# Masked softmax on one core: an empty first turn around the work of VectorE and ScalarE

## The chip, the core and the metric

The kernel runs on one core of a Trainium2 chip. The core has five engines with an instruction stream each: TensorE (PE), VectorE (DVE), ScalarE (ACT), GpSimd (POOL) and SyncE (SP), and 16 DMA engines that move data between the chip's memory (HBM) and the core's own. The engines run on their own and wait for each other on semaphores. The metric is the time of one execution on the device in microseconds; the median of several runs is compared.

## The reference

The input x has 16 batches of 8 heads x 256 x 256 numbers in float32, and each batch has a length between 128 and 255. The softmax goes along the last axis over the first `length` columns; the other columns of the result are zero.

```python
result = np.zeros_like(x)
for b in range(batch):
    length = lengths[b]
    masked = x[b, :, :, :length].copy()
    masked = masked - np.max(masked, axis=-1, keepdims=True)
    exp_masked = np.exp(masked)
    result[b, :, :, :length] = exp_masked / np.sum(exp_masked, axis=-1, keepdims=True)
```

## The kernel before

A batch is 2048 rows of 256 columns, held as 128 partitions x 16 rows x 256 (2 MB). Eight such slots stand in `xt`, and batch number b (in the kernel's own order) uses slot b modulo 8. Each slot is worked on in place: it is loaded, masked, exponentiated, divided and stored.

**The start.** ACT's queue loads the 16 lengths (L139), SP's queue the first batch in two halves (L142). POOL makes a row of column numbers, `iota_i` (L177), two vectors of ones and two zeros. DVE turns the column numbers into `down` (L225), casts the lengths (L230), PE spreads them over the partitions with a small matmul (L210), and DVE scales them into `len_s` (L233). POOL waits for both of DVE's steps, clears the right part of one slot (L187), then issues the loads of the next three batches (L192) and clears three slots more.

**Loads.** From batch 4 on, a loop on POOL (L197 to L205) reads a batch's length and picks, over nested branches, a load as wide as the length needs (L164); it waits for the load before last, and for the store that frees the slot.

**DVE.** Its stream is written out: `begin`-like steps L223 to L237, then the masks of batch 0 (`mask`, L242), then for each batch `divide` of the first half, the mask of the next batch, `divide` of the second half. `mask` waits for the load and takes the minimum of x and a ramp that is huge and negative behind the length (a `scalar_tensor_tensor` of 128 x 2048); `divide` waits for a half batch of exponentials, takes the reciprocal of the row sums (L263) and multiplies (L266). Masks count on the semaphore `s_min`, half batches of exponentials on `s_exp`, divided halves on `s_out`.

**ACT.** After one exponential on a zero, which brings its table in (`warm`, L342), a loop of two turns (L345) has the work of eight batches written out in its body: for each batch 16 exponentials of 128 x 256, each with its row sum (L354), 128 in a turn. The exponentials wait for `s_min` at a value computed from the turn (L349, L351).

**Stores.** SP waits for `s_out` and stores a batch in one to four parts (L145 to L153). Before the second store it waits for the third mask (L148).

**The end.** DVE checks all row sums for values out of range (L298 to L309); a slower path stands behind a branch (L314 on DVE, L361 on ACT) and isn't taken here. SP waits for the last store.

The lines that the change touches are SP's wait L148, the start of DVE's stream (L223 to L237), its main loop (L273 to L285), and ACT's warm-up and loop (L342 to L357).

Of the kernel before, what the change touches and what calls it, by code (L numbers as in the profile page):

```python
# [9 lines left out]
F32 = mybir.dt.float32  # L10
BF16 = mybir.dt.bfloat16
I32 = mybir.dt.int32
ALU = mybir.AluOpType
AX = mybir.AxisListType.X
EXP = mybir.ActivationFunctionType.Exp
DVE = mybir.EngineType.DVE
ACT = mybir.EngineType.Activation
# [4 lines left out]
def kernel(  # L22
# [6 lines left out]
    nc = tc.nc  # L29
    P = nc.NUM_PARTITIONS  # L30

    batch, heads, seq_q, seq_k = x.shape
    rows = heads * seq_q
    assert rows % P == 0
    nt = rows // P
    half = nt // 2
# [8 lines left out]
    slots = 8  # L45
# [3 lines left out]
    def batch_of(pos):  # L49
        return pos + 1 if pos < ahead - 1 else {ahead - 1: 15, 15: 0}.get(pos, pos)  # L50
# [5 lines left out]
    big = 1.0e30  # L56

    def parts(b):


        if b == 0:
            cuts = [0, 2, quarter, half, nt]
        elif b < 8:
            cuts = [0, half, half + quarter, nt]
        elif b < 13 or b == batch - 1:
            cuts = [0, half, nt]
        else:
            cuts = [0, nt]
        return [slice(i, j) for i, j in zip(cuts, cuts[1:])]
# [3 lines left out]
    xt = pool.tile([P, slots, nt, seq_k], F32, name="xt")  # L73
    word64 = pool.tile([1, batch], mybir.dt.int64, name="word64")
    word = word64.bitcast(I32)
    len_b = pool.tile([1, batch], BF16, name="len_b")
    ones = pool.tile([1, P], BF16, name="ones")
    len_f = psum.tile([P, batch], F32, name="len_f")
    len_s = pool.tile([P, batch], F32, name="len_s")
    iota_i = pool.tile([P, seq_k], I32, name="iota_i")  # L80
    down = pool.tile([P, seq_k], F32, name="down")
    row_sum = pool.tile([P, slots, nt], F32, name="row_sum")
    inv_sum = pool.tile([P, batch, nt], F32, name="inv_sum")
    warm = pool.tile([P, 1], F32, name="warm")
# [20 lines left out]
    with tc.tile_critical(no_gpsimd_drain=True):  # L105
        s_word = sem("s_word")
        s_ones = sem("s_ones")
        s_lenb = sem("s_lenb")
        s_lenf = sem("s_lenf")
# [4 lines left out]
        s_iota = sem("s_iota")  # L114
        s_fill = sem("s_fill")
        s_v = sem("s_v")
        s_min = sem("s_min")
        s_exp = sem("s_exp")
# [24 lines left out]
        for b in range(batch):  # L143
            s_b = s_st[b % 2] if b < late else s_late if b < batch - 1 else s_last
            for s in parts(b):  # L145
                nc.sync.wait_ge(s_out, 2 * b + (s.stop - 1) // half + 1)
                if b == 0 and s.start == 2:
                    nc.sync.wait_ge(s_min, 3)  # L148
                if 2 <= b < late and s.start == 0:
                    nc.sync.wait_ge(s_b, 64 * (b // 2 + 1))  # L150
                nc.sync.dma_start(  # L151
                    out=out_f[batch_of(b), :, s, :], in_=xt[:, b % slots, s, :]
                ).then_inc(s_b, 16 * (1 if b == 0 else (s.stop - s.start) // quarter))  # L153
# [6 lines left out]
        def pick(v, b, slot, par, ws):  # L160
# [17 lines left out]
            iota_i, pattern=[[1, seq_k]], base=0, channel_multiplier=0  # L178
# [18 lines left out]
        with nc.Fori(0, batch // 2 - 2, 1, engines=[POOL]) as q:  # L197
            for par in range(2):
                n = 2 * q + (ahead + par)
                b = n % 15 if par == 1 else n  # L200
# [14 lines left out]
        v = 0  # L215

        def step(ins):
            nonlocal v
            v += 1
            ins.then_inc(s_v, 1)  # L220


        nc.vector.wait_ge(s_iota, 1)  # L223
        step(
            nc.vector.tensor_scalar(  # L225
                out=down, in0=iota_i, scalar1=0.5, scalar2=-big, op0=ALU.add, op1=ALU.mult
            )
        )
        nc.vector.wait_ge(s_word, 16)
        nc.vector.tensor_copy(out=len_b, in_=word[:, ::2]).then_inc(s_lenb, 1)  # L230
        nc.vector.wait_ge(s_lenf, 1)
        step(
            nc.vector.tensor_scalar(  # L233
                out=len_s, in0=len_f, scalar1=big, scalar2=None, op0=ALU.mult
            )
        )
        nc.vector.wait_ge(s_v, v)  # L237

        def clip(b, s, lo, hi):

            t = xt[:, b % slots, s, lo:hi]
            return nc.vector.scalar_tensor_tensor(  # L242
                out=t,
                in0=down[:, None, lo:hi].to_broadcast([P, s.stop - s.start, hi - lo]),
                scalar=len_s[:, batch_of(b) : batch_of(b) + 1],
                in1=t,
                op0=ALU.add,
                op1=ALU.min,
            )

        def mask(b, s):
            if b == 0:
                nc.vector.wait_ge(s_ld[s.start // half], 16)
            elif b < ahead:
                nc.vector.wait_ge(s_ld[b + 1], 16)
            else:
                nc.vector.wait_ge(s_sw[b % 2], 16 * ((b - ahead) // 2 + 1))
            clip(b, s, mid, seq_k).then_inc(s_min, 1)

        def divide(b, h):  # L260
            s = slice(h * half, (h + 1) * half)
            nc.vector.wait_ge(s_exp, 2 * b + h + 1)
            step(nc.vector.reciprocal(out=inv_sum[:, b, s], in_=row_sum[:, b % slots, s]))  # L263
            nc.vector.wait_ge(s_v, v)
            t = xt[:, b % slots, s, :]
            nc.vector.tensor_tensor(  # L266
                out=t,
                in0=t,
                in1=inv_sum[:, b, s, None].to_broadcast([P, half, seq_k]),
                op=ALU.mult,  # L270
            ).then_inc(s_out, 1)

        mask(0, slice(0, half))  # L273
        mask(0, slice(half, nt))
        for b in range(batch):


            first = b != 1
            if first:
                divide(b, 0)  # L280
            if b + 1 < batch:
                mask(b + 1, slice(0, nt))
            if not first:
                divide(b, 0)
            divide(b, 1)  # L285

# [11 lines left out]
        for k, (_, _, edge, op) in enumerate(checks):  # L300
            nc.vector.tensor_scalar(  # L301
                out=bad[:, k : k + 1],
                in0=ends[:, k : k + 1],
                scalar1=edge,
                scalar2=None,
                op0=op,
# [9 lines left out]
        with nc.vector.Else():  # L316
            with nc.Fori(0, batch, 1, engines=[DVE]) as i:
                nc.vector.wait_ge(g_ld, 16 * i + 16)
                nc.vector.scalar_tensor_tensor(
                    out=g_t,  # L320
                    in0=down[:, None, :].to_broadcast([P, nt, seq_k]),
                    scalar=len_s[:, bass.ds(i, 1)],
                    in1=g_t,
                    op0=ALU.add,
                    op1=ALU.min,
# [3 lines left out]
                    out=neg_max, in_=g_t, op=ALU.max, axis=AX, negate=True  # L329
# [5 lines left out]
                    out=g_t,  # L335
                    in0=g_t,
# [2 lines left out]
                ).then_inc(g_out, 1)  # L339


        nc.scalar.activation(out=warm, in_=nc.const_aps.tensor(0.0, (P, 1), F32), func=EXP)  # L342


        with nc.Fori(0, batch // slots, 1, engines=[ACT]) as turn:  # L345
            for slot in range(slots):
                for h in range(2):
                    if slot == 0:
                        nc.scalar.wait_ge(s_min, (slots + 1 - h) * turn + (h + 1))  # L349
                    elif h == 0:  # L350
                        nc.scalar.wait_ge(s_min, slots * turn + (slot + 2))  # L351
                    for j in range(h * half, (h + 1) * half):
                        e = xt[:, slot, j, :]
                        ins = nc.scalar.activation(  # L354
                            out=e, in_=e, func=EXP, accum_out=row_sum[:, slot, j : j + 1]
                        )
                    ins.then_inc(s_exp, 1)  # L357

        nc.scalar.wait_ge(s_redo, 1)
        a_redo = length(ACT, redo_bits[0:1, 0:1])  # L360
        with nc.scalar.If(a_redo >= 1):  # L361
# [4 lines left out]
            with nc.Fori(0, batch, 1, engines=[ACT]) as i:  # L366
                nc.scalar.dma_start(out=g_t, in_=x_g[:, bass.ds(i, 1)]).then_inc(g_ld, 16)
                nc.scalar.wait_ge(g_v, 3 * i + 2)
                with nc.Fori(0, nt, 1, engines=[ACT]) as t:
                    e = g_t[:, bass.ds(t, 1), :]  # L370
                    nc.scalar.activation(
                        out=e,
                        in_=e,
                        func=EXP,
                        bias=neg_max[:, bass.ds(t, 1)],
                        accum_out=sum_g[:, bass.ds(t, 1)],
# [38 lines left out]
```

## Time and profile before

| | us |
|---|---|
| median of 3 runs | 155.04 |
| lowest and highest | 154.67 and 155.57 |
| the profiled execution | 155.4 |
| its span, first to last instruction | 153.8 |
| DVE busy | 117.1 |
| ACT busy | 105.4 |
| POOL busy | 21.3 |

The profile counts an engine as busy while it works on data. Branches, register instructions, semaphores and the issuing of DMAs are not counted; where the trace names them, the engine has a q behind it (DVEq, ACTq, SPq, POOLq: the instruction stream of the engine). "Idle" in a row is the time that the engine stood still just before, and the name behind the arrow is what ended it; "issue" there is a wait for nothing that the profile shows. q0, q1 and q10 are the DMA queues of POOL, SP and ACT, and q14 is the queue that brings instructions. The page has the span in 40 slices of 3.85 us with a digit for the busy tenths of each.

### The profile page before, as it was taken

The page shows a single profiled execution, that of the slowest core. Times are in us where ns is not written, and L with a number is a line of the kernel's source. Part 1 is how long each engine was busy: PE and PEld are TensorE (multiplying, and loading weights), DVE is VectorE, ACT ScalarE, POOL GpSimd, SP SyncE. Part 2 cuts the span into 40 slices and gives each one's busy share as a digit, 9 for nine tenths or more (in the row PEclk, how much of TensorE's full clock was granted, in tenths as well). Part 3 has the DMA queues.
Part 4 walks back from the last instruction along what each step waited for, and adds up shares of the span by engine and source line. Part 5 has one row for each costly group of instructions (what it writes and reads, how often), then busy time and mean ns, then how long its engine had stood idle before and what let it go on. Part 6 is the DMA issues. An engine that isn't in the chain of part 4 may idle for free.

```text
span 153.8 us, 950 instructions
## 1 busy us (share of the span) xinstructions
PE 0.3 (0%) x2; PEld 0.2 (0%) x2; DVE 117.1 (76%) x91; ACT 105.4 (69%) x514; POOL 21.3 (14%) x29
## 2 busy tenths in 40 slices
PE   0000000000000000000000000000000000000000
PEld 0000000000000000000000000000000000000000
DVE  1249889989979797979797797979749619747870
ACT  3088799679695959595959669594935915918800
POOL 4964000003030200202020030202002000000000
DMA  4999999999999999999999999999999999997995
GB/s 113 420 435 430 425 412 354 425 454 405 406 397 393 412 412 415 421 407 407 413 417 421 401 416 406 418 413 416 418 421 417 417 415 422 420 442 328 439 379 234
DMA packets 10646, 61.57 MB, mean 400 GB/s; under 512 B 898, under 2 KB 1010, under 8 KB 7058
## 3 DMA queue, kind: packets, MB, share of 16 engines
q1 hardware_dynamic: 5904, 35.65, 56.6%
q0 software_dynamic: 4736, 25.89, 41.6%
q14 instruction: 4, 0.03, 0.1%
q10 hardware_dynamic: 2, 0.00, 0.0%
HBM read 27.98 MB, written 33.55 MB: 400 GB/s over the span
## 4 chain that ended last, share of the span: by engine, by line
DMA 43%; DVE 32%; ACT 17%; issue 2%; POOL 1%; SPq 1%; PE 0%; POOLq 0%; ACTq 0%
DMA xt<-in_x_dram 23%; DMA out_dram<-xt 20%; ACT xt L354 17%; DVE xt L266 16%; DVE xt L242 13%; DVE inv_sum L263 1%; SPq L151 1%; POOL xt L187 1%; DMA word<-in_lengths_dram 1%; DVE ends L298 0%; POOL xt L192 0%; DVE bad L301 0%; DVE len_s L233 0%; PE len_f L210 0%; PE count L212 0%
## 5 line engine op out<-in xcount | busy, mean ns | idle before, releaser
L354 ACT ACTIVATE xt<-xt 128x256 f32<-128x256 f32 x256 | 102.4, 402 | 38.3 <-DVE xt L242 38.3
L266 DVE TENSOR_TENSOR xt<-xt,inv_sum 128x2048 f32<-128x2048 f32 x32 | 73.3, 2292 | 1.1
L242 DVE SCALAR_TENSOR_TENSOR xt<-down,len_s,xt 128x2048 f32<-128x2048 f32 (+1 forms) x17 | 37.8, 2222 | 15.7 <-DMA xt<-in_x_dram 15.7
L354 ACT ACTIVATION_READ_ACCUMULATOR xt<-xt 128x1 f32 x256 | 48.1, 188 | 0.0
L164 POOL DMA_DIRECT2D xt<-in_x_dram x12 | 13.3, 1106 | 93.6 <-DMA out_dram<-xt 90.3
L263 DVE RECIPROCAL inv_sum<-row_sum 128x8 f32<-128x8 f32 x32 | 6.3, 198 | 12.7 <-ACT xt L354 12.7
L187 POOL MEMSET xt<- 128x1536 f32 x4 | 5.4, 1399 | 1.1 <-DVE len_s L233 1.1
L342 ACT ACT_TABLE_LOAD x1 | 1.3, 1283 | 1.6 <-SPq L105 1.6
L192 POOL DMA_DIRECT2D xt<-in_x_dram x3 | 1.8, 591 | 0.0
L225 DVE TENSOR_SCALAR down<-iota_i 128x256 f32<-128x256 int32 x1 | 0.3, 301 | 1.6 <-POOL iota_i L177 1.6
L298 DVE TENSOR_REDUCE ends<-inv_sum 128x1 f32<-128x256 f32 x2 | 0.7, 412 | 0.0
L230 DVE CAST len_b<-word 1x16 bf16<-1x16 int32 x1 | 0.2, 163 | 0.4 <-DMA word<-in_lengths_dram 0.4
L212 PE MATMUL count<-bad,ones_c 128*1 128x3 bf16 x1 | 0.2, 165 | 146.2 <-DVE bad L301 146.2
L233 DVE TENSOR_SCALAR len_s<-len_f 128x16 f32<-128x16 f32 x1 | 0.2, 174 | 0.4 <-PE len_f L210 0.4
L177 POOL IOTA iota_i<- 128x256 int32 x1 | 0.3, 332 | 0.6 <-SPq L105 0.6
L309 DVE TENSOR_REDUCE redo<-count 1x1 f32<-1x3 f32 x1 | 0.1, 148 | 0.3 <-PE count L212 0.3
L301 DVE TENSOR_SCALAR bad<-ends 128x1 bf16<-128x1 f32 x3 | 0.3, 150 | 0.0
L212 PEld LDWEIGHTS count<-bad,ones_c 128*1 128x1 bf16 x1 | 0.1, 79 | 146.3 <-DVE bad L301 146.3
L183 POOL MEMSET seed<- 1x1 f32 x2 | 0.2, 226 | 0.0
L342 ACT ACTIVATE warm<-const-float32-0.0 128x1 f32<-128x1 f32 x1 | 0.2, 203 | 0.0
L180 POOL MEMSET ones<- 1x128 bf16 x1 | 0.2, 195 | 0.0
L210 PE MATMUL len_f<-len_b,ones 1*128 1x16 bf16 x1 | 0.2, 168 | 2.7 <-DVE len_b L230 2.7
(8 smaller groups left out, 0.8 us busy)
## 6 DMA issues: line engine op xcount, KB each, us to landing
out_dram<-xt SPq DMA_DIRECT2D x20, 1024.0 KB
xt<-in_x_dram POOLq DMA_DIRECT2D x4, 2048.0 KB, 17.0
out_dram<-xt SPq DMA_DIRECT2D x15, 512.0 KB
xt<-in_x_dram POOLq DMA_DIRECT2D x3, 1728.0 KB, 17.7
out_dram<-xt SPq DMA_DIRECT2D x2, 2048.0 KB
xt<-in_x_dram POOLq DMA_DIRECT2D x2, 1600.0 KB, 19.9
xt<-in_x_dram POOLq DMA_DIRECT2D x2, 1280.0 KB, 15.3
xt<-in_x_dram SPq DMA_DIRECT2D x2, 1024.0 KB, 7.0
```

The source lines that it names most:

```text
L151: nc.sync.dma_start(out=out_f[batch_of(b), :, s, :], in_=xt[:, b % slots, s, :]).then_inc(s_b, 16 * (1 if b == 0 else (s.stop - s.start) / ...
L164: nc.gpsimd.dma_start(out=xt[:, slot, :, :w], in_=x_n[:, b, :, :w]).then_inc(s_sw[par], 16)
L177: nc.gpsimd.iota(iota_i, pattern=[[1, seq_k]], base=0, channel_multiplier=0).then_inc(s_iota, 1)
L187: nc.gpsimd.memset(xt[:, b, :, low:], 0.0).then_inc(s_fill, 1)
L192: nc.gpsimd.dma_start(out=xt[:, b], in_=x_f[batch_of(b)]).then_inc(s_ld[b + 1], 16)
L212: nc.tensor.matmul(count, lhsT=ones_c, rhs=bad, start=True, stop=True).then_inc(s_count, 1)
L242: return nc.vector.scalar_tensor_tensor(out=t, in0=down[:, None, lo:hi].to_broadcast([P, s.stop - s.start, hi - lo]), scalar=len_s[:, batc ...
L263: step(nc.vector.reciprocal(out=inv_sum[:, b, s], in_=row_sum[:, b % slots, s]))
L266: nc.vector.tensor_tensor(out=t, in0=t, in1=inv_sum[:, b, s, None].to_broadcast([P, half, seq_k]), op=ALU.mult,).then_inc(s_out, 1)
L298: step(nc.vector.tensor_reduce(out=ends[:, k : k + 1], in_=values, op=op, axis=AX))
L342: nc.scalar.activation(out=warm, in_=nc.const_aps.tensor(0.0, (P, 1), F32), func=EXP)
L354: ins = nc.scalar.activation(out=e, in_=e, func=EXP, accum_out=row_sum[:, slot, j : j + 1])
```

## The change

DVE's work, from its first step to the last `divide`, is put into a loop of two turns. The body is cut into four parts of four batches each, and each part stands in a condition that holds from turn 1 on; the steps of the start are in the first part. In turn 0 no condition holds, so DVE jumps over all four parts and comes back to the top. ACT's loop gets one turn more, three in all, and its body is cut in the same manner into four parts of two batches. Since ACT's turns now count from one instead of zero, the waits on `s_min` would come out eight or nine too high; the warm-up exponential adds nine to `s_min`, the constants in ACT's waits are shifted to match, and SP's one wait on `s_min` is raised by nine. What is computed, and in which order, stays as it was.

```diff
@@ SP
                 if b == 0 and s.start == 2:
-                    nc.sync.wait_ge(s_min, 3)
+                    nc.sync.wait_ge(s_min, slots + 1 + 3)
@@ DVE
-        nc.vector.wait_ge(s_iota, 1)
-        step(
-            nc.vector.tensor_scalar(
-                out=down, in0=iota_i, scalar1=0.5, scalar2=-big, op0=ALU.add, op1=ALU.mult
+        def begin():
+            nc.vector.wait_ge(s_iota, 1)
+            step(
+                nc.vector.tensor_scalar(
+                    out=down, in0=iota_i, scalar1=0.5, scalar2=-big, op0=ALU.add, op1=ALU.mult
+                )
             )
...
-        mask(0, slice(0, half))
-        mask(0, slice(half, nt))
-        for b in range(batch):
...
-            first = b != 1
-            if first:
-                divide(b, 0)
-            if b + 1 < batch:
-                mask(b + 1, slice(0, nt))
-            if not first:
-                divide(b, 0)
-            divide(b, 1)
+        with nc.Fori(0, 2, 1, engines=[DVE]) as turn:
+            for group in range(0, batch, 4):
+                with nc.vector.If(turn >= 1):
+                    if group == 0:
+                        begin()
+                        mask(0, slice(0, half))
+                        mask(0, slice(half, nt))
+                    for b in range(group, group + 4):
+                        first = b != 1
+                        if first:
+                            divide(b, 0)
+                        if b + 1 < batch:
+                            mask(b + 1, slice(0, nt))
+                        if not first:
+                            divide(b, 0)
+                        divide(b, 1)
@@ ACT
-        nc.scalar.activation(out=warm, in_=nc.const_aps.tensor(0.0, (P, 1), F32), func=EXP)
+        nc.scalar.activation(out=warm, in_=nc.const_aps.tensor(0.0, (P, 1), F32), func=EXP).then_inc(
+            s_min, slots + 1
+        )
-        with nc.Fori(0, batch // slots, 1, engines=[ACT]) as turn:
-            for slot in range(slots):
-                for h in range(2):
-                    if slot == 0:
-                        nc.scalar.wait_ge(s_min, (slots + 1 - h) * turn + (h + 1))
-                    elif h == 0:
-                        nc.scalar.wait_ge(s_min, slots * turn + (slot + 2))
...
+        with nc.Fori(0, batch // slots + 1, 1, engines=[ACT]) as turn:
+            for first in range(0, slots, 2):
+                with nc.scalar.If(turn >= 1):
+                    for slot in range(first, first + 2):
+                        for h in range(2):
+                            if slot == 0:
+                                nc.scalar.wait_ge(s_min, (slots + 1 - h) * turn + (1 + 2 * h))
+                            elif h == 0:
+                                nc.scalar.wait_ge(s_min, slots * turn + (slot + 3))
```

More of the change, by code (lines that the diff above doesn't have):

```diff
@@ L220, in step @@
             ins.then_inc(s_v, 1)
-        nc.vector.wait_ge(s_iota, 1)
-        step(
-            nc.vector.tensor_scalar(
-                out=down, in0=iota_i, scalar1=0.5, scalar2=-big, op0=ALU.add, op1=ALU.mult
-            )
[L228 to L234, printed above, removed]
-            )
-        )
-        nc.vector.wait_ge(s_v, v)
+        def begin():
[4 more added lines that the diff above has]
+                )
+            )
+            nc.vector.wait_ge(s_word, 16)
+            nc.vector.tensor_copy(out=len_b, in_=word[:, ::2]).then_inc(s_lenb, 1)
+            nc.vector.wait_ge(s_lenf, 1)
+            step(
+                nc.vector.tensor_scalar(
+                    out=len_s, in0=len_f, scalar1=big, scalar2=None, op0=ALU.mult
+                )
+            )
+            nc.vector.wait_ge(s_v, v)
         def clip(b, s, lo, hi):
@@ L339 @@
                 ).then_inc(g_out, 1)
-        nc.scalar.activation(out=warm, in_=nc.const_aps.tensor(0.0, (P, 1), F32), func=EXP)
-        with nc.Fori(0, batch // slots, 1, engines=[ACT]) as turn:
-            for slot in range(slots):
-                for h in range(2):
-                    if slot == 0:
-                        nc.scalar.wait_ge(s_min, (slots + 1 - h) * turn + (h + 1))
-                    elif h == 0:
-                        nc.scalar.wait_ge(s_min, slots * turn + (slot + 2))
[L352 to L357, printed above, removed]
+        nc.scalar.activation(out=warm, in_=nc.const_aps.tensor(0.0, (P, 1), F32), func=EXP).then_inc(
+            s_min, slots + 1
+        )
+        with nc.Fori(0, batch // slots + 1, 1, engines=[ACT]) as turn:
[7 more added lines that the diff above has]
+                                nc.scalar.wait_ge(s_min, slots * turn + (slot + 3))
+                            for j in range(h * half, (h + 1) * half):
+                                e = xt[:, slot, j, :]
+                                ins = nc.scalar.activation(
+                                    out=e,
+                                    in_=e,
+                                    func=EXP,
+                                    accum_out=row_sum[:, slot, j : j + 1],
+                                )
+                            ins.then_inc(s_exp, 1)
         nc.scalar.wait_ge(s_redo, 1)
```

## The prediction

> **What bounds the kernel now.** I read the page's engine totals and the 40 slices first, then the DMA total and the chain's shares.
>
> ```profile
> span 153.8 us, 950 instructions
> PE 0.3 (0%) x2; PEld 0.2 (0%) x2; DVE 117.1 (76%) x91; ACT 105.4 (69%) x514; POOL 21.3 (14%) x29
> ...
> DMA  4999999999999999999999999999999999997995
> ...
> HBM read 27.98 MB, written 33.55 MB: 400 GB/s over the span
> ...
> DMA 43%; DVE 32%; ACT 17%; issue 2%; POOL 1%; SPq 1%; PE 0%; POOLq 0%; ACTq 0%
> ```
>
> No engine is busy more than 76% of the span, while the 16 DMA engines stand at nine tenths or more from the second slice to the end but for a few slices. 27.98 + 33.55 = 61.5 MB have to pass. So what the change is worth depends on whether it leaves the DMA engines without work. The busy time cut into stages shows where they are:
>
> ```profile
> core 0: us, PE busy (x) PEld busy (x) DVE busy (x) ACT busy (x) POOL busy (x), PEclk, DMA share, GB/s
> 0.00:2.50 2.50, 0.00 (x0) 0.00 (x0) 0.45 (x2) 0.86 (x1) 0.92 (x10) 1.00 0.16 30
> 2.50:84.00 81.50, 0.17 (x1) 0.10 (x1) 67.22 (x50) 62.53 (x307) 15.77 (x15) 1.00 1.01 411
> 84.00:136.50 52.50, 0.00 (x0) 0.00 (x0) 38.55 (x27) 35.52 (x176) 4.61 (x4) 1.00 1.02 417
> 136.50:145.50 9.00, 0.00 (x0) 0.00 (x0) 7.33 (x6) 6.49 (x32) 0.00 (x0) 1.00 0.92 391
> 145.50:153.80 8.30, 0.17 (x1) 0.08 (x1) 3.58 (x9) 0.00 (x0) 0.00 (x0) 1.00 0.76 316
> ```
>
> From 2.5 to 136.5 us the DMA share is 1.01 to 1.02: there the time is bytes over rate, and a late instruction on an engine costs nothing as long as transfers are queued. The DMA engines are short of work only before 2.5 us and in the tail, where (1 - 0.92) x 9.0 + (1 - 0.76) x 8.3 = 2.7 us are lost. The tail starts when the last load lands. The waits say the same of the engines:
>
> ```profile
> ACT xt L354 <- DVE xt L242: 38.3, 16, 5.3
> DVE xt L242 <- DMA xt<-in_x_dram: 15.7, 8, 3.6
> DVE inv_sum L263 <- ACT xt L354: 12.7, 14, 0.9
> ```
>
> ACT waits only for DVE's masks, DVE for loads and exponentials. Neither has a wait for "issue", that is, for its own instruction stream. So the change has no stall of this kind to remove, and what remains is what its extra turn costs at the start.
>
> **The start, step by step.** The timeline of the first microseconds, and the row of the branch that sets DVE free:
>
> ```profile
> L410 DVEq COMPARE_BRANCH  x1: 51/51/51, 1.0 to 1.0; - x1
> ```
>
> ```profile
> 1.09 0.52 ACTq L139 DMA_DIRECT2D word<-in_lengths_dram  x1
> 1.13 0.86 SPq L142 DMA_DIRECT2D xt<-in_x_dram  x2
> ...
> 1.61 0.30 DVE L225 TENSOR_SCALAR down<-iota_i 128x256 f32<-128x256 int32 x1 [1.61 <-POOL iota_i L177]
> ...
> 2.35 0.16 DVE L230 CAST len_b<-word 1x16 bf16<-1x16 int32 x1 [0.44 <-DMA word<-in_lengths_dram]
> ...
> 2.87 0.17 DVE L233 TENSOR_SCALAR len_s<-len_f 128x16 f32<-128x16 f32 x1 [0.35 <-PE len_f L210]
> 2.94 0.20 ACT L342 ACTIVATE warm<-const-float32-0.0 128x1 f32<-128x1 f32 x1
> 3.10 1.39 POOL L187 MEMSET xt<- 128x1536 f32 x1 [1.15 <-DVE len_s L233]
> 4.42 1.76 POOL L192 DMA_DIRECT2D xt<-in_x_dram  x3
> ...
> 7.99 0.42 ACT L354 ACTIVATE xt<-xt 128x256 f32<-128x256 f32 x1 [4.85 <-DVE xt L242]
> ```
>
> DVE's extra turn stands ahead of L225. DVE is free at 1.05 us, L225 starts at 1.61, and after it DVE has 0.44 us to spare before L230. So 0.56 + 0.44 = 1.0 us of extra turn is free. What is beyond that moves L230, the matmul, L233, POOL's fill (3.10) and POOL's three loads (4.42), one for one.
>
> Its length: one entry, four jumps taken, the turn's end with its jump back, and one compare not taken. The chain of work has POOL's branches at their pace, and the loop's own rows those of ACT's jump back:
>
> ```profile
> 115.05 0.05 POOLq L169
> 115.10 0.12 issue
> 115.22 0.11 POOLq L164
> ```
>
> ```profile
> L345 ACTq FUSED_REGOPS  x2: 50/52/55, 1.8 to 68.7; - x2
> ...
> L345 ACTq COMPARE_BRANCH  x2: 40/45/50, 68.4 to 143.1; - x2
> ```
>
> A branch and what follows it take 0.17 us on POOL, and ACT's jump back 0.3 us (68.4 to 68.7). So entry 0.1 + four jumps 0.7 + turn's end 0.3 + one compare 0.1 = 1.2 us; DVE's branch took 51 ns against ACT's 45, so some 1.35 us. Less the 1.0 free, L230 comes 0.2 to 0.4 us late, and POOL's first load with it. [...]
>
> What such a delay costs is read from the DMA queues between 0 and 7.5 us, 7.5 and 8 us, and 8 and 9 us (q1 is SP's, q0 POOL's):
>
> ```profile
> q1 hardware_dynamic: 253, 1.94, 68.9%
> ```
>
> ```profile
> q0 software_dynamic: 9, 0.15, 70.6%
> q1 hardware_dynamic: 25, 0.13, 62.8%
> ```
>
> ```profile
> q0 software_dynamic: 25, 0.41, 95.5%
> q1 hardware_dynamic: 9, 0.02, 6.1%
> ```
>
> POOL's packets begin after 7.5 us, some 3.1 us behind the issue at 4.42, just when the two loads of SP (2.1 MB) run out: 1.94 MB are through by 7.5. The 0.15 MB left would last 0.15 / 0.41 = 0.35 us. So POOL's load has some 0.3 us of cover, and a delay of 0.2 to 0.4 us leaves the DMA engines idle 0 to 0.1 us. This is the one place where DVE's start reaches the end; a longer delay would come through in full.
>
> **The other parts.** ACT's extra turn follows the warm-up exponential in order but its branches do not wait for it; ACT is idle 4.85 us before its first exponential at 7.99, so 1.2 us are hidden there. If that cover were gone, the first stores would be late, but POOL's loads would keep the DMA engines full for many microseconds (the share is 1.01 from 2.5 on), so the price is bounded by 0 and the 1.2 us and I take 0. Later, each part ends with a jump and starts with a compare: on DVE three times, on ACT three times a turn, some 0.3 us each. They stand in the stream behind a 2.29 us product or behind queued exponentials: before, ACT's jump back at 68.4 was taken while the engine worked on. If the branches did wait for the engine, 3 x 0.3 us on DVE would still fall where the DMA share is 1.02. The increment of s_min by nine on the warm-up and the waits raised by nine add no instruction: ACT's first wait now also covers its own warm-up, which ends at 3.14. SP's one raised wait, ahead of batch 0's second store, has the same cause as before, the third mask. Nothing else is moved, on POOL or PE.
>
> **Sum.** 0 to 0.1 us on a profiled execution of 155.4 us (span 153.8 and 1.6 around it). That execution stands 0.36 us above the median of 155.04; on the median I forecast 155.1 us. A difference under 0.5% (0.78 us) is about what these runs, 154.67 to 155.57, can tell from none.
>
> **Rivals.**
> A, slower: the jumped-to code is not there. In the whole span code came by DMA four times:
>
> ```profile
> q14 instruction: 4, 0.03, 0.1%
> ```
>
> ```profile
> q14 instruction: 1, 0.01, 1.9%
> ```
>
> The second row is one of them, between 15 and 16 us: 1.9% of 16 engines in 1 us is 0.3 us for a packet. Bounds for one missing piece: 0.3 us, the packet alone, and 7.0 us, SP's first loads under full traffic in the median (the row below). The nearest row is the small lengths transfer at the same moment, 1.24 us from issue to landing, which I take. One miss on DVE adds 1.24 us to 1.35: L230 is 1.6 us late, and 1.6 - 0.3 = 1.3 us of empty DMA engines carry through to the end: 156.3 us. Two misses: 157.6. It decides from a DVE turn of about 2.1 us on (1.0 free, 0.3 cover, 0.78 to count).
>
> ```profile
> xt<-in_x_dram SPq DMA_DIRECT2D x2, 1024.0 KB, 7.0
> ```
>
> ```profile
> 1.09 1.24 DMA word<-in_lengths_dram
> ```
>
> For it: parts are jumped over one after another within a microsecond, faster than code was ever walked through before. Against it: DVE's stream is about a hundred instructions, and ACT jumped back over 128 exponentials and their 128 accumulator reads at 68.4 us and went on within 0.3 us. [...] On ACT even two misses, 2.5 us, would stay under the 4.85.
>
> B, faster: a start that shifts a little puts loads ahead of stores, and the last load lands sooner. DVE waits for it:
>
> ```profile
> 136.51 2.35 DVE L242 SCALAR_TENSOR_TENSOR xt<-down,len_s,xt 128x2048 f32<-128x2048 f32 x1 [1.94 <-DMA xt<-in_x_dram]
> ```
>
> If it came the full 1.94 us sooner the tail would fill with stores, up to the 2.7 us lost there: 153.1; half of it, 154.1. For it: the tail is the only stage with something to win. Against it: the order of loads is paced by slots and stores, which the change leaves alone. It decides from 0.8 us of earlier landing.
>
> C, no jump at all, the parts merely wrapped: the built program has a compare with a branch ahead of each of four parts on DVE and on ACT, so they are there; it would end at 155.0 as well.
>
> **How the numbers follow.** Forecast with C, within 0.5%: 0.52. A: 0.30, two thirds of it one miss. B: 0.18. So faster 0.18, same 0.52, slower 0.30. The range goes from 154.1, half of B, to 157.0, which leaves out two misses; what is left out is about 0.1 above and 0.09 below. The forecast's own range is 154.6 to 155.7.
>
> **What would show it.** L226 (the old L225) starting at 2.3 to 2.6 us instead of 1.61, POOL's first load at 4.6 to 4.8, the first q0 packets before 8.1, and a DMA share still at 1.0 from 8 us on: then the steps hold. More q14 packets in the first 5 us with L226 after 3 us is A. A last load landing before 135.5 with the tail's DMA share above 0.9 is B. A wait of ACT or DVE for "issue" at a part's start would prove the part boundaries wrongly costed. The prediction is wrong if DVE's turn takes over 2.1 us, or if the tail moves with the order of transfers.

## The result and the profile after

The changed kernel takes 155.75 us in the median of 20 runs (155.17 to 156.46), the kernel before 154.69 us (154.38 to 155.57). The ratio is 1.0056 with a 95% interval of 1.0038 to 1.0073: about 0.9 us slower, some 1.1 by the medians. The forecast was 155.1 us and "within 0.5%"; the time lies in the forecast range of 154.1 to 157.0, and the ratio just beyond the bound of 0.5%, on the slower side. The forecast was built on a median of 155.04 us for the kernel before, which has 154.69 here, so the cost is the fairer comparison: 0 to 0.1 us forecast, 0.9 to 1.1 measured. Most runs of the changed kernel lie near 155.3 or near 156.2 us; the profiled one took 156.4.

The page of the changed kernel, first its span, DMA slices and code packets, then the row of GB/s of the kernel before:

```profile
span 154.5 us, 982 instructions
...
DMA  4999999999999999999999999999999999999991
GB/s 112 416 369 424 404 420 401 424 433 428 399 394 406 413 414 413 419 414 413 409 412 418 407 418 406 414 419 414 418 416 420 422 416 420 423 447 428 416 426 53
...
q14 instruction: 4, 0.03, 0.1%
```

```profile
GB/s 113 420 435 430 425 412 354 425 454 405 406 397 393 412 412 415 421 407 407 413 417 421 401 416 406 418 413 416 418 421 417 417 415 422 420 442 328 439 379 234
```

Two slices stand out: the third (7.7 to 11.6 us) fell from 435 to 369 GB/s, and the last from 234 to 53. The timeline of the first microseconds shows what came ahead of the third slice:

```profile
3.01 0.29 DVE L226 TENSOR_SCALAR down<-iota_i 128x256 f32<-128x256 int32 x1 [3.01 <-issue]
3.22 0.15 DVE L231 CAST len_b<-word 1x16 bf16<-1x16 int32 x1
...
3.96 1.39 POOL L187 MEMSET xt<- 128x1536 f32 x1 [2.14 <-DVE len_s L234]
5.28 1.75 POOL L192 DMA_DIRECT2D xt<-in_x_dram  x3
...
8.20 0.42 ACT L363 ACTIVATE xt<-xt 128x256 f32<-128x256 f32 x1 [5.06 <-DVE xt L243]
```

L226 starts at 3.01 us instead of 1.61, the cast at 3.22 instead of 2.35, POOL's first load is issued at 5.28 instead of 4.42. The chain of work now runs through the empty turn itself, so each of its steps can be read (start, length, what; DVEq is DVE's instruction stream):

```profile
1.31 0.06 DVEq L276
1.37 0.14 issue
1.51 0.06 DVEq L276
1.56 0.13 issue
1.70 0.06 DVEq L276
1.75 0.49 issue
2.24 0.06 DVEq L276
2.30 0.14 issue
2.44 0.05 DVEq L274
2.49 0.04 issue
2.53 0.06 DVEq L274
2.59 0.23 issue
2.82 0.04 DVEq L274
```

A jump takes 0.19 to 0.20 us, the one from the third to the fourth part 0.54, the jump back to the top 0.29. From 1.05 us, when DVE is free, to 3.01 us are 1.96 us.

The windows of the kernel before and of the changed one, between 7.5 and 10.5 us, 7.5 and 14, and 14 and 28 (the last two numbers are the DMA share and GB/s), each followed by the row of POOL's queue between 7.5 and 10.5 us (packets, MB, share of 16 engines):

```profile
7.50:10.50 3.00, 0.00 (x0) 0.00 (x0) 0.79 (x2) 2.51 (x13) 2.71 (x3) 1.00 1.06 451
7.50:14.00 6.50, 0.00 (x0) 0.00 (x0) 4.19 (x5) 5.82 (x29) 3.88 (x4) 1.00 1.03 440
14.00:28.00 14.00, 0.00 (x0) 0.00 (x0) 12.96 (x10) 12.44 (x63) 0.54 (x1) 1.00 1.00 400
```

```profile
q0 software_dynamic: 73, 1.20, 93.2%
```

```profile
7.50:10.50 3.00, 0.00 (x0) 0.00 (x0) 1.51 (x2) 2.30 (x11) 3.00 (x3) 1.00 1.04 360
7.50:14.00 6.50, 0.00 (x0) 0.00 (x0) 3.94 (x4) 5.80 (x29) 4.39 (x4) 1.00 0.99 382
14.00:28.00 14.00, 0.00 (x0) 0.00 (x0) 11.86 (x9) 11.20 (x57) 0.88 (x2) 1.00 1.01 415
```

```profile
q0 software_dynamic: 56, 0.92, 90.4%
```

Between 7.5 and 14 us the changed kernel moves (440 - 382) x 6.5 us = 0.38 MB less, at 440 GB/s 0.86 us of transfers. That is near the size of the loss, and it is as long as POOL's delay of 0.86 us. The DMA engines did not stand empty meanwhile: from 7.5 to 10.5 us their share is 1.04 against 1.06, while the rate is a fifth lower. POOL's packets, 16 KB each in both, took longer: 93.2% of 16 engines' 3 us over 73 packets are 0.61 us for one, 90.4% over 56 are 0.77. But the rows behind 14 us do not hand this on as it is: between 14 and 28 us 15 x 14 = 0.21 MB are made up. The kernel before, in this profiled execution, wasted time in its tail, waiting for the last load (a DMA share of 0.92 from 136.5 to 145.5 us); the changed one did not (1.02 there), since its last load landed 3.1 us sooner (its last mask starts at 133.41 instead of 136.51 us):

```profile
133.41 2.35 DVE L243 SCALAR_TENSOR_TENSOR xt<-down,len_s,xt 128x2048 f32<-128x2048 f32 x1 [1.95 <-DMA xt<-in_x_dram]
```

It ends with its DMA engines working off stores, the last slice at 53 GB/s, where their mean share is one tenth. So the two profiles alone do not settle it. The theories that went into the experiments: (1) the late start of POOL's loads is the loss; (2) ScalarE's own empty turn is; (3) the cuts into parts, or another order of transfers at the end, are.

### The profile page after: what moved, and what is told of

Its sections match the earlier page's. It is cut to its first block, busy times and chain, and to the rows that moved or that the text cites. A ratio compares the mean times of both kernels' runs of the same rounds, so it can differ in the third digit from the quotient of the medians.

```text
span 154.5 us, 982 instructions
## 1 busy us (share of the span) xinstructions
PE 0.3 (0%) x2; PEld 0.2 (0%) x2; DVE 116.8 (76%) x91; ACT 105.3 (68%) x514; POOL 21.1 (14%) x29
## 4 chain that ended last, share of the span: by engine, by line
DMA 50%; DVE 24%; ACT 13%; issue 4%; POOL 1%; SPq 1%; DVEq 0%; POOLq 0%; PE 0%; ACTq 0%
DMA out_dram<-xt 27%; DMA xt<-in_x_dram 23%; ACT xt L363 13%; DVE xt L267 12%; DVE xt L243 10%; DVE inv_sum L264 1%; POOL xt L187 1%; SPq L151 1%; DVE ends L302 1%; POOL xt L192 0%; DVE down L226 0%; DVE bad L305 0%; DVEq L276 0%; DVEq L274 0%; DVE len_s L234 0%
## 5 line engine op out<-in xcount | busy, mean ns | idle before, releaser
L226 DVE TENSOR_SCALAR down<-iota_i 128x256 f32<-128x256 int32 x1 | 0.3, 294 | 3.0 <-issue 3.0
```

## The experiments

In each, the ratio is to the kernel before on the same chip, with its 95% interval. A start loss is worked out as above, 6.5 us x (1 - rate / 440), from the window of 7.5 to 14 us.

### The start ahead of the loop

```diff
+        begin()
         with nc.Fori(0, 2, 1, engines=[DVE]) as turn:
...
                     if group == 0:
-                        begin()
                         mask(0, slice(0, half))
```

> Both loops stay, but VectorE's three starting steps stand ahead of its loop, so the empty turn comes after them. Theory 1 (the late start): the empty turn holds back len_s, so POOL's three loads are issued at 5.28 instead of 4.42 us and the DMA engines miss 0.33 MB between 8 and 10.5 us, some 0.8 us that comes through to the end. Then here POOL's first load is issued at 4.4 us, the empty turn of about 1.9 us is hidden behind the first load (VectorE waits 3.6 us there), and the time is that of the kernel before within 0.3 us, some 154.7. Theory 2 (ScalarE's missing code: its stream stood from 2.45 to 7.49 us): no change against the changed kernel, 155.5 to 155.8. Theory 3 (the cuts into parts and the order of transfers at the end): also 155.5 to 155.8.

Measured: 1.0004 (0.9989 to 1.0020), 154.89 us. From the timeline:

```profile
4.37 1.75 POOL L192 DMA_DIRECT2D xt<-in_x_dram  x3
```

POOL's loads are back at 4.37 us, the window's rate is 432 GB/s, and the loss is gone, with both empty turns and all cuts in place. Theories 2 and 3 expected 155.5 or more. (The 0.33 MB of the expectation are 0.27 by the rows above, from 7.5 to 10.5 us.) One thing does not fit the median: the profiled execution took 155.96 us, the longest of the 12, and its last slice has 62 GB/s, as in the changed kernel, although its loads were on time.

### Each engine's loop alone

ScalarE's loop with VectorE as before, and VectorE's loop with ScalarE as before (there without the nine on `s_min`):

```diff
# act_alone: the changed warm-up, loop on ACT and SP's wait; DVE's lines as before
# dve_alone: the changed loop on DVE; ACT's lines and SP's wait as before
```

> Only ScalarE's loop has the empty turn; VectorE is as before. Theory 1: the time of the kernel before within 0.3 us, and ScalarE's stream still stands some 5 us between its third and fourth jump, with two code packets near 6 us. Theory 2: 0.6 to 1.0 us over the kernel before. Theory 3: between the two.

> Only VectorE's loop has the empty turn; ScalarE is as before. Theory 1: all of the loss, 0.6 to 1.1 us over the kernel before, POOL's first load at 5.2 to 5.3 us. Theory 2: the kernel before within 0.3 us. Theory 3: between the two.

Measured: ScalarE alone 1.0030 (1.0007 to 1.0053), 154.93 us; VectorE alone 1.0056 (1.0035 to 1.0077), 155.81 us. VectorE's loop alone has the whole loss of the change. ScalarE's lies within the 0.3 us in its median (154.93 against 154.70), though by the ratio it may cost a little: 4 of its 12 runs lie from 155.4 to 156.6. Two windows of 7.5 to 14 us, first of act_alone, then of dve_alone:

```profile
7.50:14.00 6.50, 0.00 (x0) 0.00 (x0) 3.99 (x4) 5.89 (x29) 3.83 (x4) 1.00 1.04 440
```

```profile
7.50:14.00 6.50, 0.00 (x0) 0.00 (x0) 3.96 (x4) 6.29 (x31) 4.39 (x4) 1.00 0.99 394
```

### A late VectorE without any loop

```diff
+        zeros = nc.const_aps.tensor(0.0, (P, 1), F32).to_broadcast([P, 1740])
+        nc.vector.tensor_tensor(out=scratch, in0=zeros, in1=zeros, op=ALU.mult)
         nc.vector.wait_ge(s_iota, 1)
```

> The kernel before without any loop change; ahead of VectorE's first step stands one product of 128 x 1740 zeros that nothing uses, some 1.95 us by the rate of the 128 x 2048 product (2.29 us), so that the first step starts near 3.0 us as in the changed kernel. Theory 1: POOL's first load at 5.2 to 5.3 us and 0.6 to 1.1 us over the kernel before. Theories 2 and 3: the kernel before within 0.3 us.

> As late_2us with 128 x 4352 in place of 128 x 1740, some 4.9 us, so that VectorE's first step starts near 6.1 us and POOL's first load is issued near 8.3 us, 3.9 us later than in the kernel before. Theory 1 with a loss of one for one beyond 0.1 to 0.3 us of cover: 3.6 to 3.9 us over the kernel before. If late loads are made up later: under 2 us.

Measured: with 1740 columns 1.0092 (1.0077 to 1.0106), 156.13 us, POOL's first load at 5.32 us; with 4352 columns 1.0142 (1.0122 to 1.0162), 156.96 us, POOL's first load at 8.04. The windows, in this order:

```profile
7.50:14.00 6.50, 0.00 (x0) 0.00 (x0) 3.91 (x4) 6.34 (x32) 4.39 (x4) 1.00 1.02 421
```

```profile
7.50:14.00 6.50, 0.00 (x0) 0.00 (x0) 4.26 (x4) 5.98 (x30) 6.32 (x7) 1.00 0.78 279
```

A late start without any loop costs at least as much as the change, so neither an empty turn nor a cut is needed for a loss of this size. The longer delay of 3.6 us lost 2.4 us at the start and 2.2 us in all, so it does not come through one for one. The shorter one does not fit well: its start loss is only 0.3 us, yet it costs 1.4. In its profile the last load landed late, as in the kernel before (its last mask starts at 137.24 us), and the tail had DMA engines without work (255 GB/s and a share of five tenths in the slice from 139.1 us). Why this delay meets that order of transfers and the equal one of the empty turn does not is open.

### Late loads on POOL alone

```diff
+        nc.gpsimd.memset(scratch, 0.0)          # 128 x 950
         for b in range(1, ahead):
             nc.gpsimd.dma_start(out=xt[:, b], in_=x_f[batch_of(b)]).then_inc(s_ld[b + 1], 16)
```

> The kernel before, with one clearing of 128 x 950 unused numbers on POOL between its first fill and its three loads, some 0.86 us by the 1.39 us of the 128 x 1536 fill; VectorE and ScalarE start as before. Theory 1a (POOL's loads alone carry the loss): first load issued near 5.25 us and 0.6 to 1.4 us over the kernel before. Theory 1b (VectorE's own late start carries it, through its first masks): within 0.3 us of the kernel before.

Measured: 1.0052 (1.0034 to 1.0070), 155.53 us. Here VectorE and ScalarE start as in the kernel before; only POOL's loads are late. Timeline and window:

```profile
1.61 0.30 DVE L227 TENSOR_SCALAR down<-iota_i 128x256 f32<-128x256 int32 x1 [1.61 <-POOL iota_i L178]
...
5.20 1.75 POOL L194 DMA_DIRECT2D xt<-in_x_dram  x3
```

```profile
7.50:14.00 6.50, 0.00 (x0) 0.00 (x0) 3.91 (x4) 6.34 (x32) 4.40 (x4) 1.00 0.99 376
```

This is most of the change's loss again, from 0.8 us on POOL: the loads carry it, not VectorE's masks (1a against 1b).

### The loads ahead of everything

```diff
+        for b in range(1, ahead):
+            nc.gpsimd.dma_start(out=xt[:, b], in_=x_f[batch_of(b)]).then_inc(s_ld[b + 1], 16)
         nc.gpsimd.wait_ge(s_v, 2)
...
         fill(ahead)
-        for b in range(1, ahead):
-            nc.gpsimd.dma_start(out=xt[:, b], in_=x_f[batch_of(b)]).then_inc(s_ld[b + 1], 16)
```

> The kernel before, with POOL's three loads issued ahead of its wait for VectorE and of its first fill, near 1.9 us instead of 4.4. If POOL's first packets come earlier with their issue, the DMA engines are fuller between 2.5 and 7.5 us (1.87 MB moved there against 2.1 MB at the later rate) and the time is 0 to 0.6 us under the kernel before; if the first half batch lands later because the loads share the DMA engines, no gain.

> The changed kernel with the same move of POOL's three loads. Theory 1: the empty turns then cost nothing, and the time is that of early_loads within 0.3 us. Theory 3 (the loops and cuts cost something of their own): 0.6 to 1.1 us over early_loads.

Measured: on the kernel before 0.9994 (0.9983 to 1.0004), 154.71 us; on the changed kernel 1.0011 (1.0000 to 1.0022), 154.92 us. With loads that no longer wait for VectorE the empty turns cost 0.2 us, 0.3 at most by the interval, although L226 still starts at 3.00 us there. Earlier loads gain nothing over the kernel before: between 2.5 and 7.5 us the same 374 GB/s are moved, only shared between two queues (0.31 MB by POOL's and 0.13 by SP's between 7 and 8 us).

### Two empty turns

```diff
# act_two_turns, on top of act_alone
-            s_min, slots + 1
+            s_min, 2 * slots + 2
...
-        with nc.Fori(0, batch // slots + 1, 1, engines=[ACT]) as turn:
+        with nc.Fori(0, batch // slots + 2, 1, engines=[ACT]) as turn:
...
-                with nc.scalar.If(turn >= 1):
+                with nc.scalar.If(turn >= 2):
# dve_two_turns, on top of dve_alone
-        with nc.Fori(0, 2, 1, engines=[DVE]) as turn:
+        with nc.Fori(0, 3, 1, engines=[DVE]) as turn:
...
-                with nc.vector.If(turn >= 1):
+                with nc.vector.If(turn >= 2):
```

> As act_alone, but ScalarE has two empty turns, one after the other. ScalarE's first empty turn lasts 5.9 us (1.7 to 7.6) in act_alone, of which 5.0 us pass between the third and the fourth jump. Theory 4a (that code had to be brought once, and then stays): the second turn adds some 0.8 to 1.2 us, the first exponential starts at 8.9 to 9.5 us instead of 8.1, no further 5 us, and the time is that of act_alone within 0.5 us. Theory 4b (the loop is longer than what ScalarE keeps, so each turn brings code again): the second turn stands another 4 to 5 us, and the first exponential starts at 12 to 14 us; the time goes up by 0.5 us or more if the late first store then leaves the DMA engines idle, else stays.

> As dve_alone, but VectorE has two empty turns. One turn there lasts 1.8 us. Theory 1: the second adds 1.4 to 1.8 us, POOL's first load is issued at 6.7 to 7.1 us, 2.3 to 2.7 us later than in the kernel before, and the time lies between dve_alone (0.9 us over the kernel before for 0.86 us) and late_5us (2.2 us over for 3.7 us): 1.3 to 1.9 us over, that is 156.0 to 156.6. If the loss does not grow with the delay: 155.5 to 155.8.

The constants of the waits on `s_min` are raised to match on ScalarE's side. ScalarE: 1.0012 (0.9998 to 1.0027), 154.86 us. Its chain of work shows both turns, the third and fourth jump of the first, then the start and end of the second:

```profile
2.45 0.04 ACTq L350
2.50 0.44 issue
...
3.14 4.30 issue
7.44 0.04 ACTq L350
...
7.99 0.04 ACTq L350
...
9.09 0.04 ACTq L350
```

The stream stands from 2.50 to 7.44 us in the first turn and not at all in the second, which takes 1.1 us. Theory 4a expected this of code that has to come once and then stays; no row names what ended the stop. Even a first exponential at 9.24 us, 1.25 us later than the kernel before has it, costs next to nothing.

VectorE: 1.0045 (1.0031 to 1.0059), 155.38 us, not the 156.0 to 156.6 of theory 1, and close to the 155.5 to 155.8 of a loss that does not grow. POOL's first load was issued at 6.52 us, 2.1 us late, and the window has

```profile
7.50:14.00 6.50, 0.00 (x0) 0.00 (x0) 3.93 (x4) 6.32 (x31) 4.80 (x5) 1.00 0.99 378
```

0.9 us of start loss, as in the changed kernel with a delay of 0.86. So the loss goes with what the DMA engines miss by 14 us, not with the delay. POOL's first packets (queue q0) come out at nearly the same time: between 7.5 and 8 us for issues at 4.42, 5.28 and 6.52. Here the row of q0 between 7.5 and 8 us for the last, against 9 packets for the first in the prediction:

```profile
q0 software_dynamic: 3, 0.05, 52.4%
```

Three packets took 52.4% of 16 engines' 0.5 us here, 1.4 us each; the nine of the kernel before took 70.6%, 0.63 us each.

### Both kernels once more

Nothing is edited here: second profiles of the kernel before and of the changed kernel.

> The kernel before, for a second profile of it: the first one's execution took 155.4 us, 0.7 over its median. In act_two_turns (154.8 us, start untouched) the DMA engines moved 60.41 MB by 148 us and its last slice has 154 GB/s. Theory 1 expects the same of a typical execution of the kernel before, 154.5 to 154.9 us: as much moved by 14 us as in its first profile, and no single engines finishing a microsecond after the others (last slice over 130 GB/s).

> The changed kernel, for a second profile: its executions lie near 155.3 and near 156.2 us, and the first profile was of the upper kind, with 53 GB/s in its last slice. Theory 1 expects the lower kind, if it is met, to have the same loss between 7.5 and 14 us, some 0.3 to 0.4 MB, and a last slice over 130 GB/s; the upper kind has the same loss at the start and 50 to 65 GB/s in the last slice. If the lower kind has no loss at the start, theory 1 is wrong.

Measured: the kernel before 1.0002 (0.9989 to 1.0016), its profiled execution again above its median (155.5 us); the changed one 156.3 us in its two runs, the upper kind (1.0110, 1.0080 to 1.0139). Their windows of 7.5 to 14 us, before first:

```profile
7.50:14.00 6.50, 0.00 (x0) 0.00 (x0) 4.12 (x5) 5.71 (x29) 3.83 (x4) 1.00 1.03 441
```

```profile
7.50:14.00 6.50, 0.00 (x0) 0.00 (x0) 3.86 (x4) 5.89 (x29) 4.39 (x4) 1.00 0.98 377
```

The start loss repeats (0.94 us), and the changed kernel's last slice again has a low DMA share (one tenth and 72 GB/s, against three tenths and 153; 50 to 65 were expected). A profile of the lower kind, near 155.3, was not met. But the other profiles tell the two apart. "MB" is what the DMA engines had moved from the start of the span to 130 us, from the row of all DMA packets in that stretch:

| profiled execution | POOL's first loads | MB | last slice, GB/s | time, us |
|---|---|---|---|---|
| act_two_turns | on time | 52.75 | 154 | 154.83 |
| early_loads | early | 52.70 | 152 | 154.82 |
| pool_late | 0.8 us late | 52.49 | 156 | 155.25 |
| dve_two_turns | 2.1 us late | 52.43 | 156 | 155.36 |
| begin_ahead | on time | 52.66 | 62 | 155.96 |
| after_again | 0.9 us late | 52.47 | 72 | 156.30 |
| the changed kernel | 0.9 us late | 52.52 | 53 | 156.38 |

These are single executions. Of those that end alike, the ones with late loads take 0.4 to 0.5 us more. A last slice of 53 to 72 GB/s goes with another 0.9 to 1.1 us, and it comes with loads on time too. The two profiles of the kernel before (52.65 and 52.61 MB) end in a third way: their last load landed late, and their last masks start at 136.51 and 135.74 us.

## Why the prediction was right, and where it was not

**The bound** held. Transfers set the time (a DMA share of 1.02 from 28 to 148 us), and the engines have slack (VectorE, the busiest, has 76% of the span): the delay that counted is the one of POOL's first loads, at the place named, behind SP's. pool_late and begin_ahead show it from both sides. But the price of 0 to 0.1 us was too low by far. Of the signs named, the first q0 packets came before 8.1 us (7.6), while L226 (3.01 us against 2.3 to 2.6), POOL's first load (5.28 against 4.6 to 4.8) and the DMA share (0.97 from 8 to 14 us) missed. That the time still lies in the range is in part luck: its slow side was there for rival A, and the loss came without it.

**The length of VectorE's turn** was the first mis-sized term: 1.35 us forecast, 1.96 measured. The jumps took 0.20 instead of 0.17 us, and one of them 0.54; the entry took 0.26 instead of 0.1. The jump of 0.54 comes at the same place in begin_ahead, where it lies 1.9 us later (0.53 us), so it is not bound to the traffic of the moment. But in the second empty turn of dve_two_turns the same jump takes 0.26 us (3.27 to 3.53), and that whole turn 1.24 us (L226 starts at 4.25 us there, at 3.01 in dve_alone) against 1.59 for the first (1.31 to 2.90): the first pass is the dear one. No code packet lies beside it, and its cause stays open. The length of the branch instruction did not give the time of a taken jump here: the trace has 0.05 to 0.06 us for the instruction and 0.19 to 0.20 from one taken jump to the next.

**The free 1.0 us** ahead of the cast held: 1.96 - 1.0 = 0.96, measured 0.87 at the cast and 0.86 at POOL's load.

**The cover of 0.3 us** was the second. It was read as the bytes that SP still had to move when POOL's packets began, after which the DMA engines would be idle. But POOL's packets begin at 7.6 us with either issue time, and the engines' share hardly falls (1.04 against 1.06 up to 10.5 us); what the late issue changes is how long the first packets take, 0.77 us in the mean up to 10.5 us instead of 0.61, and so how many follow. So 0.86 us late missed 0.86 us of transfers by 14 us, not 0.56, and 2.1 us late missed 0.9. Why a packet of the same size takes longer then was not shown.

**"A longer delay would come through in full"** fell: 3.6 us cost 2.2, and 2.1 us cost 0.7.

**ScalarE's turn** was said to last 1.2 us and cost nothing. By the medians it cost some 0.2 us in act_alone, act_two_turns and begin_ahead, and only in act_alone does the interval stay clear of no cost (0.07 to 0.53%). But the reason given was not the one: it lasted some 6 us, and ended near the time when the first mask did (7.7 us). The first exponential came at 8.20 us, 0.5 behind that mask, and 0.2 later than before.

**Rival A**, missing code, fits ScalarE and not VectorE, where it would have counted. ScalarE stood 4.9 us, four times the 1.24 taken and inside the bounds of 0.3 and 7.0, and code came meanwhile: two packets between 5.5 and 6 us in the changed kernel, in act_alone one, at 5.9 us (two were expected). In act_two_turns the second turn went over the same code without a stop, in 1.1 us. That the code is what the stop waited for was not shown. VectorE's longest stop was 0.49 us (1.75 to 2.24); its loop alone brings a code packet too, at 6.4 us in dve_alone, but its empty turn is over by then.

**Rival B** gave nothing. The last load landed 3.1 us sooner than in the profile before and the tail filled with stores, as that rival wanted, but the time did not fall. Nor is the shift shown to come from the change: in act_two_turns and early_loads, with loads on time and 154.8 us, the last mask starts at 131.82 and 129.31 us, so it is the two profiled executions of the kernel before, each some 0.7 us over its median, that stand out. **Part boundaries** cost nothing that can be measured, as forecast (begin_ahead has them all).

**The sum.** 0.86 us missed by 14 us and 0.9 us of measured loss look like one number, but that they agree is in part luck. Of the bytes missed at the start some are made up: by 130 us the late profiles of the table lack 0.14 to 0.32 MB against those with loads in time, 0.3 to 0.8 us at the 417 GB/s of the span's middle. That is the loss of the changed kernel's faster runs (155.2 to 155.4 us against 154.69), and nearly that of pool_late (0.8) and dve_two_turns (0.7). The slower runs, 8 of 20 above 156.0, lose about 0.9 us more, and both that were profiled end with a DMA share of one tenth in the last slice. Late loads neither suffice for this tail nor are they needed: begin_ahead has it in its profiled run, its only one above 155.9, and act_alone has 2 of 12 runs above 155.9, pool_late and dve_two_turns none of 6 each. What decides it is not known, and the records do not tell the 16 engines apart. late_2us (0.3 us missed by 14 us, 1.4 lost) ends with its last load late, as the two profiles of the kernel before do.

## What to carry to other kernels

When transfers are the bound, look for the one moment where the next transfer's issue hangs on an engine, and keep everything away from the instructions ahead of it; the same empty turn placed three instructions later was free (a ratio of 1.0004 against 1.0056). Size such a turn from branches that are taken on the same engine, and allow for a first pass over a jump that costs more, as here (0.54 against 0.26 us). A delay was worth what the DMA engines missed and did not make up, which can be less than the delay (2.2 us for 3.6, 0.7 for 2.1); and a median over two kinds of runs, here two ways to end, is no measure of the start alone.

## What the runs showed that was not expected

- ScalarE stood 4.9 to 5.1 us at the third jump of its first empty turn while loads were running, in every run that has this turn, and not at all in a second pass over the same code.
- POOL's first packets follow the issue by 4.0 us (issued at 1.93), 3.2 (4.42), 2.3 (5.28) or 1.4 (6.52 and 8.04): the longer, the more of SP's 2.1 MB is still ahead (1.5 MB for the issue at 4.42, 1.1 for that at 5.28).
- Two nearly equal delays of POOL's loads (0.9 and 0.8 us), by an idle product on VectorE and by a clearing on POOL, cost 0.92% and 0.52%, with intervals that do not meet.
